# Experts' combining products one pair later, and sums of squares taken by ScalarE, in a two-block network on one core

## The chip, the core and the metric

The kernel is one program on one NeuronCore of a Trainium2 chip. The metric is device time in microseconds (us) of a whole execution; lower is better. TensorE (PE in the profile) does the matrix products, PEld is its weight loading, VectorE is DVE, ScalarE is ACT, GpSimd is POOL, and SyncE (SP) issues most of the transfers between HBM and on-chip memory. TensorE accumulates into eight PSUM banks of 128 partitions by 512 float32.

## The reference

Two blocks on 512 tokens of 1024 numbers. The first block has a hyena mixer and a differential attention mixer; the second has a layer of sparse attentions and a hierarchical mixture of experts, and then a last rmsnorm. The change lies in the mixture of experts and in what surrounds it:

```python
h = rmsnorm_2(x, norm_ffn[l])
x = x + hier_moe(h, ...)            # then rmsnorm_2(x, norm_final)

def hier_moe(h, ...):
    g_logit = tok @ w_group + b_group          # 4 groups
    e_logit = tok @ w_expert + b_expert        # 32 experts, 8 to a group
    # best group, its two best experts, weights from both softmaxes
    ...
    gate, up = jnp.split(xb @ w_gate_up[e], 2, axis=-1)
    return (jax.nn.silu(gate) * up) @ w_down[e]
    # summed per token with the weights
```

All is float32. Each expert has 1024x512 gate-up weights and 256x1024 down weights, so the 32 experts' weights are 96 tiles of 1 MB.

## The kernel before, in words

The program is written as if in one stream; the tile framework gives each operation to its engine, simulates a schedule when the program is built, and from that writes a fixed order of instructions for each engine. Each engine then runs its own order strictly in sequence, and waits by semaphores. `tc.issue_after(ins)` binds what is written inside it to stand behind `ins` in its engine's order. So the orders can move at places that the code's text does not touch.

**Router (lines 1834 to 1946).** Eight steps `m`, one for each block of 128 of the 1024 columns, take the last projection of the attention layer (`pg`, three products of split operands a block) and add the residual into `hn`. The function `after(m)`, called one step late, makes the router's logits (`lg`), transposes `hn` back to rows by token (`tp`), which ScalarE copies into `acc` (the residual stream, 512 tokens in 4 blocks `t` of 128 rows) and VectorE into `xp`, and takes the sums of squares of each token: ScalarE squares `hn` into `sq`, and one-column products with a column of ones (`st`) sum over partitions. Behind the loop, `xd` gets `xp` by four transfers that ScalarE issues (L1871), `rs` is the reciprocal root (VectorE, VectorE, GpSimd, L1876 to 1878), `L` the scaled logits (L1886), and a chain of small VectorE operations picks the group, two experts, ranks `rk` and weights `Wd`. `wr` holds these numbers and `rs` split in a high and a low part (`split`, L328 on ScalarE, L329 on VectorE).

**Experts (lines 1950 to 2060).** 16 pairs of experts (`N_PAIR`), two pairs to a group `g` (`NG` is 8), 64 slots an expert. `prepare(g)` finds which token each slot holds: the one-hot `P`, products `sp` with `wr`, the index `ix`, two gathers `xg` by GpSimd (L1969), and the slot weights `sw`, `sr`. `turn(j)` transposes a pair's rows (`ga`) and scales them into `Xs`. `gate_up(j)` multiplies by the raw weights: the two experts of a pair use the two halves of the array's columns, one 64-wide product each (`gu`, 16 products). `act(j)` transposes the result (`T`) and makes `H`; `down(j)` makes 8 such 64-wide products (`dn`), splits the weighted result into `yh` (ScalarE, L2037) and `yl` (VectorE, L2038), together `Y[j]`, and makes the one-hot `PT[j]` by a product with `sel` (L2041). `combine(g)` brings the outputs of a group's two pairs back to rows by token: 8 blocks of 4 full-width products each (`cb`, L2052), added into `acc` by VectorE (L2055). The `cb` products share two PSUM banks with `sp` and `sel`. The main loop writes, for each pair `j`: `prepare` of the next group (even `j`), `gate_up(j)`, `turn(j+1)`, `down(j-1)`, four blocks of `combine`, `act(j)`; `combine(g-1)` begins in the step that also holds the `down` of its own last pair.

**Weights.** SyncE loads the 96 tiles in order of use (L223, L232); 12 are loaded ahead, and each later one takes a buffer when the products that read it are done.

**Tail.** The last pair's `down`, the last `combine`, then for each block `t` square, power, scale (L2094 to 2097) and the output's transfer. `overflow` (L2106) counts, on VectorE, experts with over 64 tokens, and SyncE reads that count (L2124) for a loop that runs no times with these inputs.

Of the kernel before, what the change touches and what calls it, by code (L numbers as in the profile page):

```python
# [10 lines left out]
FT = mybir.dt.float32  # L11
# [9 lines left out]
D = 1024  # L21
# [1765 lines left out]
def moe(k, A, C, out, ctx, mhp, mh, ml):  # L1787
# [36 lines left out]
    with tc.tile_pool(name="mo1", bufs=2, reuse_waits="tile") as wk, tc.tile_pool(name="mo1x", bufs=1, reuse_waits="tile") as xp, \  # L1824
# [9 lines left out]
        st = pp.tile([128, 4, KD], FT, name="st")  # L1834

        def after(m, hn, hh, hl, sq):
# [12 lines left out]
            xv = xp_[:, :, 512 * h:512 * h + 512].rearrange("p t (a f) -> p t f a", a=4)[:, :, 32 * q:32 * q + 32]  # L1849
            nc.vector.tensor_copy(xv, tp.rearrange("p t (f a) -> p t f a", a=4))  # L1850
        pend = None
        for m in range(KD):
            h2 = wk.tile([128, 512], FT, name="h2", bufs=3)
            nc.scalar.dma_start(h2, k.hdram[:, m, META:])
            if m % 2 == 0:
                wh, wl = k.W.get()
            ps = pp.tile([128, 512], FT, name="pg", bufs=2)
            mm_split(nc, [ps], wh, wl, mh, ml, [slice(0, 512)], KD, slice(128 * (m % 2), 128 * (m % 2) + 128))
            if pend:
                after(*pend)  # L1860
# [7 lines left out]
            pend = (m, hn, hh, hl, sq)  # L1868
# [7 lines left out]
        nc.vector.tensor_reduce(rs, st, AX.X, OP.add)  # L1876
# [50 lines left out]
        nc.vector.tensor_tensor(rk, rk, rp[:, 0:4], OP.add)  # L1927
# [9 lines left out]
        nc.vector.tensor_tensor(Wd, Wd, o2, OP.add)  # L1937
        wp = Wd.rearrange("p t (j e) -> p t j e", e=2)
# [10 lines left out]
    with tc.tile_pool(name="mo2", bufs=2, reuse_waits="tile") as wk, tc.tile_pool(name="mo2y", bufs=1, reuse_waits="tile", side="right") as yp, \  # L1949
# [3 lines left out]
        def prepare(g):  # L1953

            P = wk.tile([128, 4, 4, 64], FR, name="P", bufs=1)
            nc.vector.tensor_tensor(P, rk[:, :, 4 * g:4 * g + 4, None].to_broadcast([128, 4, 4, 64]),
                                    iota[:, None, None, :].to_broadcast([128, 4, 4, 64]), OP.is_equal)
            sp = pp.tile([128, 2, 8], FT, name="cb", bufs=2)
            for j in range(2):
                for t in range(4):  # L1960
                    nc.tensor.matmul(sp[:, j], P[:, t, 2 * j:2 * j + 2].rearrange("p e s -> p (e s)"),
                                     wr[:, t, 2 * g + j], start=(t == 0), stop=(t == 3))
            s8 = wk.tile([128, 2, 8], FT, name="s8")
            nc.vector.tensor_copy(s8, sp)
            ix = wk.tile([128, 2], I32, name="ix")
            nc.vector.tensor_copy(ix, sp[:, :, 6])
            for j in range(2):
                x = XG[2 * g + j] = wk.tile([128, D], FT, name="xg", bufs=3)
                nc.gpsimd.indirect_dma_start(out=x, out_offset=None, in_=xd[:, :],  # L1969
                                             in_offset=bass.IndirectOffsetOnAxis(ap=ix[:, j:j + 1], axis=0))  # L1970
            s3 = wk.tile([128, 2, 3], FT, name="s3")
            nc.gpsimd.tensor_tensor(s3, s8[:, :, 0:6:2], s8[:, :, 1:6:2], OP.add)
            w, r = (wk.tile([128, 2], FT, name=n, bufs=3) for n in ("sw", "sr"))
            for i, a in enumerate((slice(0, 64), slice(64, 128))):
                nc.gpsimd.tensor_copy(w[a], s3[a, :, i])
            nc.gpsimd.tensor_copy(r, s3[:, :, 2])
            SW[g] = (w, r)
# [23 lines left out]
        def gate_up(j):  # L2001
# [4 lines left out]
            for c in range(2):  # L2006
                ws = [k.W.get_raw() for _ in HALF]
                for a in range(4):
                    kk = 4 * c + a
                    for o, w in zip(HALF, ws):  # L2010
                        nc.tensor.matmul(ps[o], xs[:, kk, o], w[:, a], start=(kk == 0), stop=(kk == 7))  # L2011
            G[j] = wk.tile([128, 512], FT, name="G")
            nc.scalar.activation(G[j], ps, AF.Copy, scale=SW[g][1][:, i:i + 1])

        def act(j):
# [9 lines left out]
            nc.vector.scalar_tensor_tensor(H[j], th, 0.5, tp[:, 2:4], op0=OP.mult, op1=OP.mult)  # L2025

        def down(j):
            ps = pp.tile([128, 2, 512], FT, name="dn")
            h = H.pop(j)
            ws = [k.W.get_raw() for _ in HALF]  # L2030
# [4 lines left out]
            w = SW[j // 2][0][:, j % 2:j % 2 + 1]  # L2035
            yh, yl = (yp.tile([128, 2, 512], FR, name=n, bufs=3) for n in ("yh", "yl"))
            nc.scalar.activation(yh, ps, AF.Copy, scale=w)  # L2037
            nc.vector.scalar_tensor_tensor(yl, ps, w, yh.bitcast(FT), op0=OP.mult, op1=OP.subtract)  # L2038
            Y[j] = (yh, yl)
# [3 lines left out]
            nc.vector.tensor_scalar(PT[j], b, col64, None, op0=OP.is_equal)  # L2043

        def combine(g):
            for t in range(4):
                for i in range(2):
                    ps = pp.tile([128, 512], FT, name="cb", bufs=2)
                    n = 0
                    for j in (2 * g, 2 * g + 1):  # L2050
                        for y in Y[j]:
                            nc.tensor.matmul(ps, PT[j][:, t * 128:t * 128 + 128], y[:, i], start=(n == 0), stop=(n == 3))  # L2052
                            n += 1
                    a = acc[:, t, 512 * i:512 * i + 512]
                    nc.vector.tensor_tensor(a, a, ps, OP.add)  # L2055
                    yield

# [7 lines left out]
        for j in range(N_PAIR):  # L2065
# [10 lines left out]
            steps(nxt, 2)  # L2076
            steps(comb, 4)
            act(j)
# [3 lines left out]
        for _ in combine(NG - 1):  # L2082
            pass


    with tc.tile_pool(name="mo3", bufs=2, reuse_waits="tile") as wk:
# [13 lines left out]
        overflow(k, A, rt, cm, rk, Wd, rs, cnt, xd, acc, last_norm)  # L2100


def overflow(k, A, rt, cm, rk, Wd, rs, cnt, xd, acc, last_norm):
# [4 lines left out]
    nc.vector.tensor_scalar(x, cnt, 64.0, None, op0=OP.is_gt)  # L2108
# [128 lines left out]
```

## Time and profile before

| what | value |
| --- | --- |
| time, median of 3 executions | 2403.26 us (2397.03 to 2406.48) |
| profiled execution | 2399.58 us, its span 2397.8 us |
| TensorE busy over the span | 94% |
| VectorE, ScalarE, GpSimd busy | 64%, 45%, 30% |
| granted TensorE clock, mean | 0.965 of full speed |
| HBM traffic over the span | 278.19 MB read, 25.58 MB written |

The profile is one execution recorded in hardware. Times count from the start of its span. A product of two float32 operands stands in it as two records, so `gu` and `dn` groups count two records a product, while `cb` (operands rounded for the fast float32 form) has one; a few records are missing. "A <- B" in the waits means that A waited and B's end released it. The rows that follow further down are from the last 400 us, the only part in which the two kernels differ.

### The profile page before, as it was taken

How to read it: one execution, taken by the hardware profiler on the slowest of the kernel's cores; microseconds unless marked ns; L12 is line 12 of the kernel's file. 1: busy time of each engine (PE TensorE's matmuls, PEld its weight loads, DVE VectorE, ACT ScalarE, POOL GpSimd, SP SyncE). 2: the span in 40 equal slices, each digit the busy share in tenths (PEclk: the TensorE clock that was granted, in tenths of full speed). 3: DMA queues.
4: the chain of work that ended last, by engine and by line, in shares of the span. 5: the costliest groups of instructions: out<-in, count | busy, mean ns of one | idle time of the engine just before them, and what ended most of it. 6: DMA issues, size and time to landing. Idle time of an engine off the chain costs nothing. (4 is left out here: it accounts for less than half of the span.)

```text
span 2397.8 us, 37215 instructions
## 1 busy us (share of the span) xinstructions
PE 2258.6 (94%) x14396; PEld 1844.0 (77%) x14396; DVE 1536.0 (64%) x2845; ACT 1068.5 (45%) x2164; POOL 710.5 (30%) x709
## 2 busy tenths in 40 slices
PE   7999999998999989999999989899999999799997
PEld 6989999997889888888898869887666667344333
DVE  7778764537985587787767744678678554433333
ACT  5666654433344466566656644435444432121111
POOL 3455540115642333333323325432011021101000
PEclk9999999999999899999999989898999999799998
DMA  6333322223127422111111225532121336699871
GB/s 225 125 108 111 113 93 89 88 71 105 56 85 217 142 62 71 53 54 53 58 49 54 71 89 173 179 82 64 62 75 53 115 103 236 254 423 372 330 299 45
DMA packets 242061, 306.19 MB, mean 128 GB/s; under 512 B 20648, under 2 KB 208436, under 8 KB 233306
## 3 DMA queue, kind: packets, MB, share of 16 engines
q1 hardware_dynamic: 203328, 245.90, 30.6%
q10 hardware_dynamic: 33002, 32.64, 4.5%
q0 software_dynamic: 5552, 25.25, 2.9%
q8 instruction: 114, 1.87, 0.3%
q14 instruction: 65, 0.53, 0.1%
HBM read 278.19 MB, written 25.58 MB: 127 GB/s over the span
## 5 line engine op out<-in xcount | busy, mean ns | idle before, releaser
L263 POOL TENSOR_TENSOR wlo<-wraw,whi 128x1024 fp32r<-128x1024 f32 (+1 forms) x91 | 181.0, 1997 | 479.2 <-ACT whi L282 346.7
L263 DVE TENSOR_TENSOR wlo<-wraw,whi 128x1024 fp32r<-128x1024 f32 (+2 forms) x201 | 225.5, 1135 | 148.7 <-ACT whi L282 141.1
L282 ACT CAST whi<-wraw 128x1024 fp32r<-128x1024 f32 x198 | 206.0, 1047 | 169.9 <-PE ps L813 50.2
L811 PE MATMUL ps<-xh,whi 128*128 128x264 f32 x1024 | 214.0, 286 | 3.4 <-ACT hTd L584 3.0
L813 PE MATMUL ps<-xl,whi 128*128 128x264 f32 x1024 | 213.9, 286 | 0.0
L815 PE MATMUL ps<-xh,wlo 128*128 128x264 f32 x1024 | 211.8, 285 | 0.0
L811 PE MATMUL pj<-xh,whi 128*128 128x512 f32 (+2 forms) x544 | 193.9, 359 | 5.0 <-DVE rr L1193 4.6
L815 PE MATMUL pj<-xh,wlo 128*128 128x512 f32 (+2 forms) x544 | 191.2, 354 | 0.5 <-DVE wlo L263 0.5
L813 PE MATMUL pj<-xl,whi 128*128 128x512 f32 (+2 forms) x544 | 191.4, 354 | 0.0
L811 PEld LDWEIGHTS ps<-xh,whi 128*128 128x128 f32 x1024 | 160.5, 189 | 5.8 <-ACT hTd L584 4.0
L813 PEld LDWEIGHTS ps<-xl,whi 128*128 128x128 f32 x1024 | 161.2, 189 | 1.6 <-issue 1.3
L815 PEld LDWEIGHTS ps<-xh,wlo 128*128 128x128 f32 x1024 | 160.8, 189 | 1.2 <-issue 0.8
L813 PE MATMUL pj<-vx,whi 128*128 128x256 f32 (+1 forms) x480 | 136.6, 286 | 0.0
L1302 ACT ACTIVATE p<-S,mx 128x528 f32<-128x528 f32 x128 | 89.6, 702 | 77.5 <-DVE mx L1300 42.6
L811 PEld LDWEIGHTS pj<-xh,whi 128*128 128x128 f32 x544 | 104.8, 193 | 19.9 <-DVE rr L1193 6.0
L815 PEld LDWEIGHTS pj<-xh,wlo 128*128 128x128 f32 x544 | 104.0, 192 | 13.7 <-DVE wlo L263 0.7
L813 PEld LDWEIGHTS pj<-xl,whi 128*128 128x128 f32 x544 | 104.4, 193 | 12.6
L2011 PE MATMUL gu<-wraw,Xs 128*64 128x512 f32 x400 | 112.1, 626 | 0.0
L1300 DVE TENSOR_REDUCE mx<-S 128x1 f32<-128x528 f32 x128 | 88.9, 700 | 13.6 <-PE S L1299 12.2
L2055 DVE TENSOR_TENSOR acc<-acc,cb 128x512 f32<-128x512 f32 x64 | 43.1, 684 | 79.6 <-PE cb L2052 79.4
L813 PEld LDWEIGHTS pj<-vx,whi 128*128 128x128 f32 x480 | 91.6, 191 | 0.0
L1298 PE MATMUL S<-ks,qh 128*128 128x264 f32 x256 | 71.9, 301 | 11.9 <-ACT p L1302 11.7
(662 smaller groups left out, 6482.7 us busy)
## 6 DMA issues: line engine op xcount, KB each, us to landing
wraw<-in_w_gate_up_dram SPq DMA_DIRECT2D x50, 1024.0 KB
wraw<-in_hy_w_in_dram SPq DMA_DIRECT2D x32, 1024.0 KB
wraw<-in_da_w_in_dram SPq DMA_DIRECT2D x32, 1024.0 KB
wraw<-in_hy_w_out_dram SPq DMA_DIRECT2D x16, 1024.0 KB
wraw<-in_da_w_out_dram SPq DMA_DIRECT2D x16, 1024.0 KB
wraw<-in_w_down_dram SPq DMA_DIRECT2D x14, 1024.0 KB
wraw<-in_w_in_dram SPq DMA_DIRECT2D x20, 512.0 KB
whi<-in_w_down_dram SPq DMA_DIRECT2D x18, 512.0 KB
```

Of the source, the lines that this page charges most:

```text
L263: eng.tensor_tensor(l, r, h.bitcast(FT), OP.subtract)
L282: nc.scalar.copy(hf, vf)
L811: nc.tensor.matmul(ps[i], wh[:, kk, fsl], xh[:, kk, c], start=f, stop=False)
L813: nc.tensor.matmul(ps[i], wh[:, kk, fsl], xl[:, kk, c], start=False, stop=False)
L815: nc.tensor.matmul(ps[i], wl[:, kk, fsl], xh[:, kk, c], start=False, stop=l)
L1298: nc.tensor.matmul(S[:, i, 0:TH], qh[:, qs], ks[:, c], start=True, stop=False)
L1300: nc.vector.tensor_reduce(mx[:, m:m + 1], S[:, :, 0:TH], AX.XY, OP.max, negate=True)
L1302: nc.scalar.activation(p.rearrange("p (a b) -> p a b", a=2), S[:, :, 0:TH], AF.Exp, bias=mx[:, m:m + 1], accum_out=sm[:, m:m + 1])
L2011: nc.tensor.matmul(ps[o], xs[:, kk, o], w[:, a], start=(kk == 0), stop=(kk == 7))
L2055: nc.vector.tensor_tensor(a, a, ps, OP.add)
```

## The change

Six edits, all in the mixture of experts and its edges:

1. The `st` products and the eight squarings of `hn` go. ScalarE squares `acc` by token instead, with a running sum: four blocks of 896 columns ahead of the last `after`, four of 128 behind it; one addition replaces the reduction.
2. VectorE's part of the split of `rs` stands behind the ranks.
3. `prepare(0)` works by pair: half of `P`, its products, its index, its gather, then the other half. Its small sums go to VectorE.
4. In the main loop the four blocks of `combine` are bound behind the last product of `gate_up(j)` and written ahead of `down(j-1)`, so `combine(g-1)` begins one pair later. In `down` the `sel` product comes first and the loop's order is by output half; the last pair's `yh` and `yl` are made in halves.
5. `last_combine` takes eight PSUM banks: pair 14's products of the eight blocks ahead of pair 15's.
6. The overflow count's VectorE operations are bound behind `H[4]`.

```diff
-        st = pp.tile([128, 4, KD], FT, name="st")
+        st = xp.tile([128, 2, 4], FT, name="st")
+        def squares(i, c):
+            for t in range(4):
+                sq = wk.tile([128, D], FT, name="sq")
+                nc.scalar.activation(sq[:, 0:c.stop - c.start], acc[:, t, c], AF.Square, accum_out=st[:, i, t:t + 1])
...
-                nc.tensor.matmul(st[:, i, m:m + 1], sq[:, c], k.ones, start=True, stop=True)
...
-            sq = wk.tile([128, 512], FT, name="sq")
-            nc.scalar.activation(sq, hn, AF.Square)
...
+        squares(0, slice(0, D - 128))
         after(*pend)
+        squares(1, slice(D - 128, D))
...
-        nc.vector.tensor_reduce(rs, st, AX.X, OP.add)
+        nc.vector.tensor_tensor(rs, st[:, 0], st[:, 1], OP.add)
...
-        rsb = rs[:, :, None].to_broadcast([128, 4, N_PAIR])
-        split(k, rsb, wr[:, :, :, 4], wr[:, :, :, 5])
+        with tc.issue_after(last_rank.ins):
+            split(k, rsb, wr[:, :, :, 4], wr[:, :, :, 5])
...
+            for js in ((0,), (1,)) if g == 0 else ((0, 1),):
...
+            eng = nc.gpsimd if g else nc.vector
+            eng.tensor_tensor(s3, s8[:, :, 0:6:2], s8[:, :, 1:6:2], OP.add)
...
-            for a in range(2):
-                for i in range(2):
-                    for o, w in zip(HALF, ws):
-                        nc.tensor.matmul(ps[o, i], h[:, a, o], w[:, a, 512 * i:512 * i + 512], start=(a == 0), stop=(a == 1))
+            for i in range(2):
+                for a in range(2):
+                    for o, wt in zip(HALF, ws):
+                        nc.tensor.matmul(ps[o, i], h[:, a, o], wt[:, a, 512 * i:512 * i + 512], start=(a == 0), stop=(a == 1))
+                if last or i:
+                    c = slice(i, i + 1) if last else slice(0, 2)
+                    nc.scalar.activation(yh[:, c], ps[:, c], AF.Copy, scale=w)
...
+        def last_combine():
+            banks = []
+            for n, b in (("gu", 2), ("gu", 2), ("ga", 1), ("T", 1), ("cb", 2), ("cb", 2)):
+                ps = pp.tile([128, 512], FT, name=n, bufs=b)
+                t, i = divmod(len(banks), 2)
+                add(ps, t, i, N_PAIR - 2, True, False)
+                banks.append(ps)
...
-            gate_up(j)
+            done = gate_up(j)
             nxt = turn(j + 1) if j + 1 < N_PAIR else iter(())
-            steps(nxt, 1)
+            with tc.issue_after(done):
+                steps(comb, 4)
             if j:
                 down(j - 1)
             if i == 0 and g:
                 comb = combine(g - 1)
-            steps(nxt, 2)
-            steps(comb, 4)
-            act(j)
+            steps(nxt, 3)
+            hidden = act(j)
+            if j == 4:
+                late = hidden
...
-        for _ in combine(NG - 1):
-            pass
+        last_combine()
...
+    with tc.issue_after(late):
+        nc.vector.tensor_scalar(x, cnt, 64.0, None, op0=OP.is_gt)
```

Two places show how the engines' orders move. The first is TensorE's order late in the expert stage of before, from the transposes of one pair's hidden values (`T`) over the last seven down products of the pair before it to the first combining products that read those down products (`cb<-yh`, `cb<-yl`):

```order
L1994 MATMUL ga<-ident,xg 128x128 x4
L2034 MATMUL dn<-wraw,H 64x512
L2020 MATMUL T<-ident,G 128x128 x4
L2034 MATMUL dn<-wraw,H 64x512 x7
L2011 MATMUL gu<-wraw,Xs 64x512
L2052 MATMUL cb<-yh,PT 128x512 x2
L2052 MATMUL cb<-yl,PT 128x512 x2
L2011 MATMUL gu<-wraw,Xs 64x512 x7
L2052 MATMUL cb<-yh,PT 128x512
L2052 MATMUL cb<-yl,PT 128x512
```

The same stretch in the changed kernel, from the seven down products of the same kind to the first combining products that read them:

```order
L2053 MATMUL dn<-wraw,H 64x512 x7
L2041 LDWEIGHTS sel
L2041 MATMUL cb<-rkT,sel 128x512
L2022 MATMUL gu<-wraw,Xs 64x512 x8
L2053 MATMUL dn<-whi,H 64x512 x2
L2053 MATMUL dn<-wlo,H 64x512 x2
L2053 MATMUL dn<-whi,H 64x512 x2
L2053 MATMUL dn<-wlo,H 64x512 x2
L2022 MATMUL gu<-wraw,Xs 64x512 x8
L2062 MATMUL cb<-yh,PT 128x512
L2062 MATMUL cb<-yl,PT 128x512
```

Before, one gate-up product stood between the two; now sixteen gate-up and eight down products do, in runs of eight rather than of one and seven.

The second place is ScalarE's order at the end of the router loop, before:

```order
L328 CAST hh<-hn 128x512
L1867 ACTIVATE sq<-hn 128x512
L1847 COPY acc<-tp 128x4x128 x2
L1880 COPY lgs<-lg 36x512
L1871 DMA xd<-xp 128x1024 x4
L328 CAST wr<-rs 128x64
```

and in the changed kernel:

```order
L328 CAST hh<-hn 128x512
L1852 COPY acc<-tp 128x4x128 x2
L1840 ACTIVATE sq,st<-acc 128x896 x2
L1885 COPY lgs<-lg 36x512
L1840 ACTIVATE sq,st<-acc 128x896
L1876 DMA xd<-xp 128x1024 x2
L1840 ACTIVATE sq,st<-acc 128x896
L1876 DMA xd<-xp 128x1024 x2
L1840 ACTIVATE sq,st<-acc 128x128 x4
L328 CAST wr<-rs 128x64
```

Eight squarings and the four transfers' issues now stand between the last copy into `acc` and `rs`.

## Rows read from the trace of the kernel before

**Rows 1.** The page: the span and its instructions.

```profile
span 2397.8 us, 37215 instructions
```

**Rows 2.** Busy time by stage: busy us (instructions) of each engine, PEclk, DMA share, GB/s.

```profile
2000.00:2039.10 39.10, 39.10 (x209) 31.60 (x208) 13.38 (x16) 10.41 (x17) 2.40 (x1) 1.00 0.58 211
...
2068.30:2210.40 142.10, 142.10 (x629) 59.70 (x628) 50.18 (x97) 27.70 (x56) 14.97 (x28) 0.99 0.96 386
2210.40:2367.00 156.60, 147.88 (x580) 58.41 (x579) 51.92 (x93) 26.09 (x49) 6.31 (x12) 0.98 0.69 260
```

**Rows 3.** The chain that ended last, 2300 to 2324 us: start, us, what.

```profile
2300.35 1.12 ACT yh L2037
...
2301.50 1.29 DVE yl L2038
...
2303.57 5.27 PE gu L2011 x14
2308.84 1.13 PE cb L2052 x4
2309.97 1.00 PE dn L2034 x2
...
2312.11 1.87 PE dn L2034 x8
...
2316.16 2.04 PE cb L2052 x8
...
2320.33 3.58 PE gu L2011 x14
```

**Rows 4.** Waits, 2068 to 2370 us: us in total, times, longest.

```profile
PE cb L2052 <- ACT yh L2037: 4.8, 4, 1.2
...
PEld cb L2052 <- DVE acc L2055: 4.1, 5, 0.8
...
PEld gu L2011 <- DMA wraw<-in_w_down_dram: 0.4, 1, 0.4
```

**Rows 5.** Timeline of the router's end: start, us, engine; in brackets the idle time before.

```profile
2040.43 0.63 ACT L1867 ACTIVATE sq<-hn 128x512 f32<-128x512 f32 x1
...
2040.96 1.07 ACT L1847 COPY acc<-tp 128x512 f32<-128x512 f32 x2
...
2041.42 0.95 PE L1844 MATMUL st<-ones,sq 128*128 128x1 f32 x8
...
2043.36 0.15 DVE L1876 TENSOR_REDUCE rs<-st 128x4 f32<-128x32 f32 x1
...
2043.54 2.77 ACTq L1871 DMA_DIRECT2D xd<-xp  x4
...
2046.69 0.28 DVE L329 TENSOR_TENSOR wr<-rs,wr 128x64 fp32r<-128x64 f32 x1 [0.88 <-ACT wr L328]
```

**Rows 6.** Timeline from the first gather to the first gate-up product.

```profile
2057.48 1.18 POOL L1972 TENSOR_TENSOR s<-s 128x6 f32<-128x6 f32 x1 [12.64 <-DVE ix L1966]
...
2065.84 0.19 POOL L1972 TENSOR_TENSOR s<-s 128x6 f32<-128x6 f32 x1
...
2068.27 1.12 PE L2011 MATMUL gu<-wraw,Xs 128*64 128x512 f32 x2
```

**Rows 7.** Timeline of the tail.

```profile
2366.97 0.75 PE L2020 MATMUL T<-ident,G 128*128 128x128 f32 x4
...
2377.47 1.06 ACT L2094 ACTIVATE s<-acc 128x1024 f32<-128x1024 f32 x1 [3.52 <-DVE acc L2055]
...
2378.44 0.19 ACT L2094 ACTIVATION_READ_ACCUMULATOR s<-acc 128x1 f32 x1
...
2388.51 1.28 DVE L2097 SCALAR_TENSOR_TENSOR s<-acc,rf,gf 128x1024 f32<-128x1024 f32 x1 [0.66 <-POOL rf L2096]
```

**Rows 8.** Transfers of SyncE's queue after the first buffer came free.

```profile
2073.57 1.05 SPq L232 DMA_DIRECT2D wraw<-in_w_gate_up_dram  x2
```

**Rows 9.** Busy time and transfer rate within the expert stage, columns as in group 2.

```profile
2080.00:2200.00 120.00, 120.00 (x538) 52.49 (x534) 45.70 (x85) 23.98 (x47) 9.06 (x14) 1.00 1.01 414
```

More of the change, by code (lines that the diff above doesn't have):

```diff
@@ L1963, in prepare @@
             s8 = wk.tile([128, 2, 8], FT, name="s8")
-            nc.vector.tensor_copy(s8, sp)
[L1965 to L1970, printed above, removed]
+            ix = wk.tile([128, 2], I32, name="ix")
@@ new lines, in prepare @@
+            for js in ((0,), (1,)) if g == 0 else ((0, 1),):
+                c = slice(2 * js[0], 2 * js[-1] + 2)
+                n = c.stop - c.start
+                nc.vector.tensor_tensor(P[:, :, c], rk[:, :, 4 * g + c.start:4 * g + c.stop, None].to_broadcast([128, 4, n, 64]),
+                                        iota[:, None, None, :].to_broadcast([128, 4, n, 64]), OP.is_equal)
+                for j in js:
+                    for t in range(4):
+                        nc.tensor.matmul(sp[:, j], P[:, t, 2 * j:2 * j + 2].rearrange("p e s -> p (e s)"),
+                                         wr[:, t, 2 * g + j], start=(t == 0), stop=(t == 3))
+                c = slice(js[0], js[-1] + 1)
+                nc.vector.tensor_copy(ix[:, c], sp[:, c, 6])
+                for j in js:
+                    x = XG[2 * g + j] = wk.tile([128, D], FT, name="xg", bufs=3)
+                    nc.gpsimd.indirect_dma_start(out=x, out_offset=None, in_=xd[:, :],
+                                                 in_offset=bass.IndirectOffsetOnAxis(ap=ix[:, j:j + 1], axis=0))
@@ L1976, in prepare @@
-            nc.gpsimd.tensor_copy(r, s3[:, :, 2])
+                eng.tensor_copy(w[a], s3[a, :, i])
+            eng.tensor_copy(r, s3[:, :, 2])
             SW[g] = (w, r)
@@ L2043, in down, with add @@
             nc.vector.tensor_scalar(PT[j], b, col64, None, op0=OP.is_equal)
+            ps = pp.tile([128, 2, 512], FT, name="dn")
+            h = H.pop(j)
+            ws = [k.W.get_raw() for _ in HALF]
+            w = SW[j // 2][0][:, j % 2:j % 2 + 1]
+            yh, yl = (yp.tile([128, 2, 512], FR, name=n, bufs=3) for n in ("yh", "yl"))
+            last = j == N_PAIR - 1
+            for i in range(2):
[5 more added lines that the diff above has]
+                    nc.scalar.activation(yh[:, c], ps[:, c], AF.Copy, scale=w)
+                    nc.vector.scalar_tensor_tensor(yl[:, c], ps[:, c], w, yh[:, c].bitcast(FT), op0=OP.mult, op1=OP.subtract)
+            Y[j] = (yh, yl)
+        def add(ps, t, i, j, start, stop):
+            for n, y in enumerate(Y[j]):
+                nc.tensor.matmul(ps, PT[j][:, t * 128:t * 128 + 128], y[:, i], start=(start and n == 0), stop=(stop and n == 1))
         def combine(g):
@@ L2048, in combine @@
                     ps = pp.tile([128, 512], FT, name="cb", bufs=2)
-                    n = 0
                     for j in (2 * g, 2 * g + 1):
-                        for y in Y[j]:
-                            nc.tensor.matmul(ps, PT[j][:, t * 128:t * 128 + 128], y[:, i], start=(n == 0), stop=(n == 3))
-                            n += 1
+                        add(ps, t, i, j, j % 2 == 0, j % 2 == 1)
                     a = acc[:, t, 512 * i:512 * i + 512]
@@ L2056, in combine @@
                     yield
+        def last_combine():
[5 more added lines that the diff above has]
+                banks.append(ps)
+            ps = None
+            for t in range(4):
+                if t == 3:
+                    ps = pp.tile([128, 2, 512], FT, name="dn")
+                    banks += [ps[:, i] for i in range(2)]
+                    for i in range(2):
+                        add(banks[6 + i], t, i, N_PAIR - 2, True, False)
+                for i in range(2):
+                    add(banks[2 * t + i], t, i, N_PAIR - 1, False, True)
+                    a = acc[:, t, 512 * i:512 * i + 512]
+                    nc.vector.tensor_tensor(a, a, banks[2 * t + i], OP.add)
         def steps(g, n):
@@ L2099, in moe, with overflow @@
         last_norm()
-        overflow(k, A, rt, cm, rk, Wd, rs, cnt, xd, acc, last_norm)
-def overflow(k, A, rt, cm, rk, Wd, rs, cnt, xd, acc, last_norm):
+        overflow(k, A, rt, cm, rk, Wd, rs, cnt, xd, acc, last_norm, late)
+def overflow(k, A, rt, cm, rk, Wd, rs, cnt, xd, acc, last_norm, late):
     nc, tc = k.nc, k.tc
```

29 lines of the change are left out of this document (7 added, 22 removed).

## The prediction

> **What bounds the kernel now.** The table of busy times by stage comes first, since the two kernels differ only in the last 400 us of the span [rows 1]. In the router stage TensorE is busy in all 39.10 us. In the first half of the expert stage it is busy in all 142.10 us at a granted clock of 0.99, with the transfers' share at 0.96; in the second half in 147.88 of 156.60 us [rows 2]. So TensorE's own order is the bound, weights in HBM stand close behind, and 8.7 us of idle time lie in the second half. The waits say what for: combining products wait for `yh` (4 times, 1.2 us each), and only 0.4 us in all is put down to weights [rows 4].
>
> The chain that ended last gives TensorE's prices [rows 3]. A run of 8 records of down products takes 1.87 us, one of 14 gate-up records 3.58 (16 with the two that the trace lacks). The difference, 1.71 for 8 records, makes 0.854 for 4 records, that is for one product in each column half; the two halves run side by side. 1.87 less two such pairs leaves 0.17: the change from full-width products to column-half ones. The combining products show the same: 8 in 2.04, 4 in 1.13, so 0.23 each and about 0.2 for the change ahead of them. The row to learn from is the down run of 2 records, 1.00 us: one product alone in its half costs the 0.17 and then a whole 0.854, because nobody runs in the other half. Cutting a run of 8 products in 1 and 7 therefore costs one change and one half-empty pair more, 1.00 us in all; I put an odd piece at 0.427 and a change at 0.17.
>
> **Check of these prices.** I walked through TensorE's order of before from the first gate-up product with 0.427 a column-half product, 0.233 a `cb`, 0.107 a transpose, 0.21 a `sel`, 0.1 an `sp` product, and the two charges. From 2068.27 [rows 6] to the ninth pair's transposes the sum is 140.3; the trace has 142.1, the end of the first window [rows 2]. 1.5 of the difference stands in the first gate-up run at a lower clock. To the last pair's transposes at 2366.97 [rows 7] the sum is 282.9, the trace 298.7. So 14.0 us are lost after the ninth pair to something that is no work of TensorE: the 8.7 idle, some 3 in two gate-up runs behind such gaps that were granted less clock (one takes 5.27 instead of 3.58 [rows 3]), the rest in gaps too short for the table.
>
> **The expert stage, work.** The same products counted in both orders, from the first gate-up product to the last combining one: 168 changes of width before, 106 after; 38 odd pieces in 77 runs before, 18 in 47 after. The binding of four combining blocks behind `gate_up` gathers what was strewn: 62 × 0.17 = 10.5, 20 × 0.427 = 8.5, so −19.1 us (row sums 294.5 and 275.5). At the last pair's transposes the sums are 282.9 and 256.9, −26.0; 7 of it comes back behind them, since 20 more combining products (4.7 us) and some changes then stand in the tail.
>
> **The expert stage, waits.** Before, `yh` of the down just finished takes 1.12, then `yl` 1.29 [rows 3], and only one gate-up product stands between that down and the first product that reads them. After, 16 gate-up and 8 down products stand there, some 10.6 us by the prices above, against a chain of 2.4. So these waits go, and nothing takes their place in the order: what is late next is an accumulation bank, for the `acc` addition (0.8 us at the longest, 4.1 in all now [rows 4]). Between the first block of a bound group and the third, which needs its bank, lie another block and transposes or a down product, 1.6 to 3 us, more than an addition behind one other VectorE operation takes. I walked both orders with all engines' rows: it stalls in before at the places where the trace does, and in after twice, 0.4 each. That takes the 14.0 to 0.8 (bounds: 0.8, and 3.9 if the two low-clock runs stay). At the last transposes −26.0 − 13.2 = −39.2, or −36.1.
>
> **The tail.** Before, 2366.97 to 2389.79, the end of the last scaling [rows 7], is 22.8. After it carries the 4.7 and two changes more, and its products in eight banks cover the wait for the last `yh` and `yl`. My walk gives 28.0, so +5.2 (bounds +2 and +6). What follows the last scaling is the same in both. Sum for experts and tail: −34.0, or −30.9.
>
> **The router.** Before, 8 one-column records a block; in the one run that stands alone 8 take 0.95 [rows 5]. Six of eight blocks stand ahead of the last projection product, where TensorE never rests [rows 2]: 6 × 0.95 = −5.7 at the most, half of it if they hide under the transposes between them; I take −4. The squares of 512 columns (0.63 each) leave ScalarE, off its path. Against that, ScalarE's queue behind the last copy into `acc`. That copy ends at 2042.03 and `rs` starts at 2043.36, 1.33 later [rows 5]. After, four squares of 896 stand there, each 1.16 × 7/8 ≈ 1.04 from the row of 1024 with its read of the sum [rows 7], the copy of the logits (512 columns, at 0.6 as the square of 512), four issues of `xd` (2.77 together [rows 5]) and four squares of 128 at about 0.35 to 0.4: 4.2 + 0.6 + 2.8 + 1.5 = 9.1, less 1.33: +7.7. All of the routing and so the first gather queue behind `rs`; TensorE has nothing else to do there. That this undoes the gain of the first edit is the part of the change I am surest of. Two edits give some back: VectorE no longer waits 0.88 + 0.28 for ScalarE's half of the split of `rs` [rows 5], −1.1; and the first gather no longer stands behind GpSimd's sum of 1.18 (the same operation takes 0.19 where VectorE does not build `P` beside it [rows 6]), half of the position products, 0.9, and the count's operations, −2.3. Router: −4 + 7.7 − 1.1 − 2.3 = +0.3; bounds −4 and +5.
>
> The count moved behind `H[4]` costs VectorE some 3 us where it is busy a third of the time; SyncE's reading of it stands behind a load that waits for a later down product, so I cost it at nothing. If SyncE did stop there, later loads would start by as much later.
>
> **Sum.** −34.0 or −30.9, +0.3: −32 to −34, I take −33. Span 2397.8 − 33 = 2364.8, execution 2399.6 − 33 = 2366.6. The profiled execution lies 3.7 below the median, so against that: 2403.3 − 33 = 2370.
>
> **Rivals.** *Weights become the bound.* 12 of 96 tiles are in before 2073.57, when the first freed buffer is loaded [rows 8]; 84 tiles of 1.0486 MB and 14 gathers of 0.524 remain, 95.4 MB. At 414 GB/s, which stood from 2080 to 2200 [rows 9], they take 230 us and end at 2304; at the 386 of the whole first half [rows 2], 247 us and 2321. The last transposes come at about 2328 and the last down needs its tile at 2330. So the margin is 9 to 26 us. Each per cent under that 386 is 2.5 us more; at a tenth under it the end is 2348, 18 late: gain 15, time 2388. For it: loads now wait for TensorE, and a faster TensorE takes that slack. Against it: 0.4 us of waiting for weights so far. The Trainium skill, page "DMA: Bandwidth & Descriptors", section "Specifications", puts HBM to one core at about 358 GB/s; by it the last tile would land at 2340 and the time would be about 2380. This trace's 414 over 120 us stands against that limit.
>
> *The bound groups wait (slower side).* In before a combining block could stand anywhere; in after four are bound together over two banks, with two joins a pair, 28 in all. If VectorE, behind `yl` (1.29) or scalings, adds late at each join, TensorE waits there. From 33/28 = 1.2 us a join there is no gain; at 2 us it is +23 and 2426. For it, those 4.1 us in five waits; against it, VectorE is busy 50 of 142 us [rows 2].
>
> *The clock and the router.* The gaps go but low-clock runs remain or come elsewhere, and the router costs its full +5: gain 20 to 26, time about 2380.
>
> *The waits only move.* Row sums fall by 19 but stalls of some 14 arise behind `Xs` or `G` in the denser order: gain 19, time 2384.
>
> **Chances.** The forecast (2360 to 2378) 0.64; weights 0.10; clock or router 0.10; moved waits 0.06; bound groups that cost over half of the gain 0.07, more than half of them not faster at all; better than 2358 0.03. The range 2356 to 2388 leaves out little beyond the bound groups and the tail of the weights. A measurement of this kernel tells about 0.5%, 12 us, from no change: faster 0.90, same 0.06, slower 0.04.
>
> **What would show it.** Right: no wait of `cb` for `yh` or `yl` over 0.5 us; `dn` x2 pieces of 1.00 gone from most of the chain; the last pair's transposes about 260 us behind the first gate-up product (298.7 before); `rs` some 9 us behind the last `acc` copy and the first gate-up product within 4 us of 2068. Wrong: gate-up or down waiting for transfers by several us at a time, or `cb` waiting for `acc` additions at most joins.

## The result, and the profile after

The changed kernel takes 2363.97 us in the median (2362.28 to 2370.13, 4 runs) against 2401.17 for the kernel before (2397.03 to 2406.48, 4 runs): a ratio of 0.9849, 95% interval 0.9821 to 0.9876. That is 37 us less, inside the forecast range; the forecast was 2370, 33 less. A later measurement of the same two kernels (`changed_again` below) gave 2368.19 against 2400.30, 32 us less, so the size of the gain is known to some 5 us.

The page of the changed kernel begins so:

```profile
span 2360.5 us, 37091 instructions
```

Both spans can be cut at the same places of the program. Each length is the difference of two starts (or ends) of rows in the timelines: the first and the eighth `hn` of the router, the scaling of `rs`, the first gather, the first gate-up product, the last pair's transposes `T`, the end of the last output scaling, the end of the span.

| stretch | before | after | difference |
| --- | --- | --- | --- |
| start to first `hn` (same code) | 1991.7 | 1991.9 | +0.2 |
| first to eighth `hn` | 47.4 | 42.9 | -4.5 |
| eighth `hn`'s end to scaling of `rs` | 3.75 | 7.64 | +3.9 |
| `rs` to first gather | 15.3 | 12.6 | -2.7 |
| first gather to first gate-up | 9.4 | 10.6 | +1.2 |
| first gate-up to last `T` | 298.7 | 259.4 | -39.3 |
| last `T` to last scaling's end | 22.8 | 26.4 | +3.6 |
| rest | 8.0 | 8.4 | +0.4 |

The busy times by stage of the changed kernel, cut at the first gate-up product, at the ninth pair's region and at the last transposes; these answer to [rows 2]:

```profile
2000.00:2034.70 34.70, 34.70 (x161) 26.88 (x160) 12.88 (x16) 7.73 (x12) 2.40 (x1) 1.00 0.67 247
2066.25:2208.00 141.75, 141.44 (x655) 61.82 (x656) 55.29 (x119) 30.16 (x59) 14.11 (x25) 0.99 0.98 403
2208.00:2325.60 117.60, 117.57 (x528) 52.93 (x525) 44.72 (x82) 24.10 (x45) 6.12 (x12) 1.00 0.81 323
2325.60:2352.10 26.50, 18.77 (x79) 11.64 (x77) 18.33 (x29) 6.14 (x11) 2.17 (x4) 0.94 0.18 66
```

In the second half TensorE now works 117.57 of 117.60 us, at full granted clock. The 8.7 us of idle time are gone, and with them the low clock (0.98 in the second half before, 1.00 now). In the list of waits from 2066 to 2326 us no wait of a combining product (L2062) for `yh`, `yl` or `acc` is left. What is left are short waits of weight loads (PEld), of which only the three in the first line below are for a transfer, and one wait of a product itself, 0.3 us for `G`:

```profile
PEld dn L2053 <- DMA wraw<-in_w_gate_up_dram: 0.9, 3, 0.4
...
PE T L2032 <- ACT G L2024: 0.3, 1, 0.3
```

The chain that ended last, of the changed kernel, in the same phase as [rows 3]:

```profile
2210.11 3.43 PE dn L2053 x16
2213.55 3.43 PE gu L2022 x16
2216.98 2.07 PE cb L2062 x8
2219.05 0.47 PE T L2032 x4
2219.51 1.85 PE cb L2062 x8
...
2233.45 1.00 PE dn L2053 x2
...
2236.06 3.58 PE dn L2053 x14
```

Here a down run of 16 records follows a gate-up run and takes 3.43, with no change of width ahead of it, and the combining products stand in eights. Pieces of 1.00 are left, but few. No ScalarE or VectorE row stands in this part of the chain.

At the router's end ScalarE does what was foreseen, in its timeline (answering to [rows 5]), but faster:

```profile
2036.07 1.07 ACT L1852 COPY acc<-tp 128x512 f32<-128x512 f32 x2
2037.02 0.96 ACT L1840 ACTIVATE sq<-acc 128x896 f32<-128x896 f32 x1
...
2038.78 0.33 ACTq L1876 DMA_DIRECT2D xd<-xp  x1
...
2039.37 0.95 ACT L1840 ACTIVATE sq<-acc 128x896 f32<-128x896 f32 x1
...
2040.39 1.15 ACTq L1876 DMA_DIRECT2D xd<-xp  x1
2041.15 0.20 ACT L1840 ACTIVATION_READ_ACCUMULATOR sq<-acc 128x1 f32 x1
2041.59 0.31 ACT L1840 ACTIVATE sq<-acc 128x128 f32<-128x128 f32 x1 [0.25 <-ACT sq L1840]
```

The issues of `xd` lie beside the squares. The last of them runs from 2040.39 over 1.15 us, and the engine is idle 0.25 us in all of that time.

### The profile page after: what moved, and what is told of

Read it like the earlier page. It is cut to its first block, busy times and chain, and to the rows that moved or that the text cites. A ratio compares the mean times of both kernels' runs of the same rounds, so it can differ in the third digit from the quotient of the medians.

```text
span 2360.5 us, 37091 instructions
## 1 busy us (share of the span) xinstructions
PE 2219.6 (94%) x14332; PEld 1832.0 (78%) x14332; DVE 1537.9 (65%) x2852; ACT 1070.5 (45%) x2173; POOL 706.2 (30%) x705
## 3 DMA queue, kind: packets, MB, share of 16 engines
q8 instruction: 113, 1.85, 0.3%
## 5 line engine op out<-in xcount | busy, mean ns | idle before, releaser
L2022 PE MATMUL gu<-wraw,Xs 128*64 128x512 f32 x400 | 97.3, 604 | 0.0
L1298 PE MATMUL S<-ks,qh 128*128 128x264 f32 x256 | 72.0, 302 | 11.9 <-ACT p L1302 11.7
L1656 ACT ACTIVATE P<-S,mx 128x128 f32<-128x128 f32 (+3 forms) x96 | 50.3, 530 | 70.1 <-PE pt L1673 55.3
```

The source lines that it names most:

```text
L1298: nc.tensor.matmul(S[:, i, 0:TH], qh[:, qs], ks[:, c], start=True, stop=False)
L1656: nc.scalar.activation(p[:, m, 0:n], S[:, m, 0:n], AF.Exp, bias=mx[:, m:m + 1], accum_out=sm[:, m:m + 1])
L2022: mm = nc.tensor.matmul(ps[o], xs[:, kk, o], w[:, a], start=(kk == 0), stop=(kk == 7))
```

## The experiments

Times are medians; the kernel before ran beside each group: 2401.25 for the first four, 2402.77 for the next four, 2400.56 and 2400.30 for the last two groups. "Lengths" are those of the table above, from one profile each. In all kernels the start up to the first `hn` is the same code, yet it took 1989.3 to 2000.8 us from profile to profile. That spread is larger than many effects here, so effects under 5 us are read from lengths. A second profile of the changed kernel (`changed_again`) shows how well these repeat: 7.66, 12.57, 10.65, 260.25, 26.45 and 8.40 for the third to the last stretch, so 0.1 in most and 0.9 in the expert stage. That 0.9 is the granted clock in the first 10 us of the gate-up products: 0.86 in the first profile and 0.77 in the second, with TensorE busy throughout.

**Which edit carries the gain: `loop_only`**

```diff
 (kernel before)
...
-            gate_up(j)
+            done = gate_up(j)
...
-            steps(nxt, 1)
+            with tc.issue_after(done):
+                steps(comb, 4)
...
-            steps(nxt, 2)
-            steps(comb, 4)
+            steps(nxt, 3)
```

> The kernel before with the main loop's edit alone (combining blocks bound behind gate_up and begun one pair later); router, start, down and tail as before. Theory: nearly the whole gain is this edit. Its TensorE order has a row sum of 275.1 us from the first gate-up product (before 294.5, changed kernel 275.5) and 256.9 at the last pair's transposes, so these should stand 258 to 261 us behind the first gate-up product, against 298.7 and 259.4, and the time at 2366 to 2369. Rival: router, start or tail carry a good part of the 37 us; then 2375 or more.

Measured 2371.34 (ratio 0.9883, 0.9847 to 0.9919); its profiled execution 2363.43, its lengths 259.83 from the first gate-up product to the last `T` and a tail of 25.6. As the theory had it by lengths: this edit alone is -38.9 and +2.8, so 36.1 of the 37.3 us. By medians it is 30 us; the median lies 2 us above the expected 2369, which is less than the spread of the start, and the interval alone (2364 to 2382) would not rule out the rival's 2375. The lengths do.

**What in that edit: `unbound` and `bound_early`**

```diff
 (changed kernel: unbound)
-            with tc.issue_after(done):
-                steps(comb, 4)
+            steps(comb, 4)
```

> The changed kernel with the four combining blocks written at the same place but not bound behind gate_up's last product. Its order strews them as before: 165 changes of width, 42 odd pieces, row sum 295.7 (changed kernel 106, 18, 275.5), and the first combining products stand right behind the down that they read. Theory (cuts and waits, both of the order): the last transposes at 295 to 299 us behind the first gate-up product, time 2395 to 2398. Rival A (that the code begins the combine one pair later does it): 2364 to 2370. Rival B (cuts alone, no waits): 2384.

Measured 2400.07 (0.9992, 0.9971 to 1.0013): as slow as before. First gate-up to last `T` 301.4, some 2 us over what was expected. Writing the combine ahead of the down gains nothing by itself; only with the binding does it. Its chain that ended last is that of the kernel before again:

```profile
2212.14 3.15 PE dn L2053 x13
2215.29 0.01 PE gu L2022
2215.29 0.44 PE dn L2053
2215.73 0.02 issue
2215.75 1.12 ACT yh L2056
2216.88 0.02 issue
2216.90 1.29 DVE yl L2057
```

```diff
 (changed kernel: bound_early)
-            with tc.issue_after(done):
-                steps(comb, 4)
             if j:
                 down(j - 1)
             if i == 0 and g:
                 comb = combine(g - 1)
+            with tc.issue_after(done):
+                steps(comb, 4)
```

> The changed kernel with the blocks bound behind gate_up, but written behind down as before, so that a combine reads the output of the down just made. Row sum 282.3 (126 changes, 26 odd pieces), 6.8 above the changed kernel, and six waits for yh and yl of about 2 us. Theory (waits and cuts both count): 17 us slower than the changed kernel, 20 if gate-up runs behind the waits get less clock: 2381 to 2384. Rival A (cuts alone): 2371. Rival B (waits alone): 2374 to 2377.

Measured 2386.76 (0.994, 0.9918 to 0.9963), 23 above the changed kernel's median; by lengths 284.2, 24.8 more, with a tail 3.4 shorter: 21 us. Its waits from 2066 to 2340 us:

```profile
PE cb L2062 <- ACT yh L2056: 4.2, 4, 1.2
PE cb L2062 <- DVE yl L2057: 2.9, 5, 0.6
```

The row sum to the last `T` (268.8 against 256.9) gives 11.9 of the 24.8. Of the other 12.9, 7.0 are idle time of TensorE (7.3 us in the stretch against 0.3 in the changed kernel); the rest, part of it lower clock (0.98 against 0.99 over the stretch), was not taken apart. Cuts alone and waits alone are both too small; the theory was some 3 us low.

**Waits alone, the cuts left: `no_wait`**

```diff
 (kernel before)
-                        for y in Y[j]:
+                        for y in Y[2 * g]:
```

> The kernel before, but both halves of a combine read the first pair's yh and yl, so nothing waits for the down just made (this leaves the second pair's outputs out of the sum). Its order has as many cuts as before: 157 changes, 42 odd pieces, row sum 294.4 against 294.5. Theory: only waits go, so 8 to 11 us off the kernel before, 2390 to 2393. Rival A (cuts alone make the difference between the two kernels): 2401, as before. Rival B (the waits are worth all 37): 2364 to 2370.

Measured 2391.18 (0.9967, 0.995 to 0.9984), 10 less than before, with as many cuts. Of the waits of TensorE for `yh` and `yl` this is left:

```profile
PE cb L2052 <- ACT yh L2037: 1.2, 2, 0.6
```

In the stretch from the first gate-up product to the last `T` TensorE is idle 2.8 us instead of 8.7. The busy times of that stretch, of the kernel before and then of `no_wait`:

```profile
2068.27:2366.97 298.70, 289.98 (x1208) 118.11 (x1207) 102.11 (x190) 53.79 (x105) 21.31 (x40) 0.98 0.82 320
```

```profile
2068.95:2362.11 293.16, 290.37 (x1228) 124.64 (x1228) 106.39 (x195) 53.44 (x105) 21.34 (x40) 1.00 0.83 326
```

The stretch is only 5.5 shorter, and the tail 4.6 (18.2 against 22.8). But the order moved too, since the last group's combining products no longer need the last pair's outputs: 12 of them stand behind the last `T` instead of 32, so 20 more, 4.7 us at 0.233, are done ahead of it. With these the waits are worth some 10 us in the stage. Both rivals fall: the waits are worth 10 of 37.

**The price of a cut: `halves_apart`**

```diff
 (changed kernel)
-                for a in range(2):
-                    for o, wt in zip(HALF, ws):
+                for o, wt in zip(HALF, ws):
+                    for a in range(2):
```

> The changed kernel with the products of each down in the order half A, half A, half B, half B for each output half instead of A, B, A, B. The work is the same. Theory (a product runs beside its neighbour in the order only if that is in the other half, each takes 0.854): a run of 8 takes 4.27 us instead of 3.41, 13.7 us over 16 downs, less 1.4 for a slightly better order: 2376. Rival A (halves run side by side only where they alternate strictly): about 2405 to 2417. Rival B (the hardware takes products of the free half out of order): 2363.

Measured 2373.55 (2 runs); by lengths first gate-up to last `T` is 266.66, 7.3 more than in the changed kernel, though the row sum without the effect is 1.3 lower: 8.6 over 15 downs, 0.57 each, between the expected 0.85 and nothing. The chain shows why:

```profile
2205.48 1.86 PE dn L2053 x4
...
2208.95 3.58 PE dn L2053 x12
...
2218.56 0.42 PE gu L2022
2218.98 3.00 PE dn L2053 x14
...
2221.99 0.42 PE dn L2053
2222.41 3.43 PE gu L2022 x15
```

A down alone between full-width work takes 1.86 + 3.58 = 5.44, against 1.00 + 3.58 in the same place of the changed kernel: 0.86 more, one product, as priced. A down between two gate-up runs pays about half of it: in this chain the gate-up run of 14 records, the down of 16 and the gate-up run of 16 take 10.45 us (2215.40 to 2225.85), and by the prices 9.99 without the effect. At both ends of that down the rows of 0.42 alternate between down and gate-up, so its first and last product run beside a gate-up product. Both rivals fall; "an odd piece costs 0.427" holds where full-width work stands on both sides.

**The weights: `no_low`**

```diff
 (changed kernel)
-            for n, y in enumerate(Y[j]):
-                nc.tensor.matmul(ps, PT[j][...], y[:, i], start=(start and n == 0), stop=(stop and n == 1))
+            nc.tensor.matmul(ps, PT[j][...], Y[j][0][:, i], start=start, stop=stop)
```

> The changed kernel without the combining products of yl (leaves out the low part of the split). TensorE's row sum falls from 275.5 to 251.2, the last transposes from 256.9 to 239.2. Theory: weights still come in time (in the changed kernel the last load is issued at 2298 and at 420 GB/s all loads could end sooner), so about 24 us faster, 2338 to 2343. Rival: transfers become the bound; TensorE waits several us for weights and the time is 2346 to 2356.

Measured 2352.34 (2 runs), the rival's time, but not by its mechanism. By lengths: 246.1 and a tail of 23.4, so 13.3 + 3.0 = 16.3 gained of 24.3 us of work. Waits for weights stay small in the whole stage, though the transfers run at their highest rate for 190 us:

```profile
PEld dn L2053 <- DMA wraw<-in_w_gate_up_dram: 1.5, 5, 0.4
...
PEld gu L2022 <- DMA whi<-in_w_gate_up_dram: 0.5, 2, 0.2
```

Its busy times in two windows, with clock, transfers' share and GB/s at the end:

```profile
2110.00:2210.00 100.00, 98.54 (x444) 40.22 (x444) 46.74 (x102) 22.45 (x44) 10.40 (x18) 1.00 1.02 423
2210.00:2300.00 90.00, 89.11 (x395) 35.66 (x391) 37.05 (x70) 20.07 (x39) 6.13 (x12) 1.00 1.02 423
```

3.6 of the missing 8 us are in the tail, where VectorE's additions and the norm set the end; 4.4 are in the expert stage. There TensorE is idle 2.7 us instead of 0.3, most of it in short waits on VectorE and ScalarE, and the first 10 us were granted 0.74 of the clock instead of 0.86, which is 1.2 us; about 1 us is left unexplained.

**The four smaller edits: `old_squares`, `old_start`, `old_tail`, `squares_early`**

```diff
 (changed kernel: old_squares)
+                nc.tensor.matmul(st[:, i, m:m + 1], sq[:, c], k.ones, start=True, stop=True)
...
+            nc.scalar.activation(sq, hn, AF.Square)
...
-        squares(0, slice(0, D - 128))
...
-        squares(1, slice(D - 128, D))
...
 (changed kernel: old_start)
-        with tc.issue_after(last_rank.ins):
-            split(k, rsb, wr[:, :, :, 4], wr[:, :, :, 5])
...
+        split(k, rsb, wr[:, :, :, 4], wr[:, :, :, 5])
...
-            for js in ((0,), (1,)) if g == 0 else ((0, 1),):
+            for js in ((0, 1),):
...
-            eng = nc.gpsimd if g else nc.vector
+            eng = nc.gpsimd
 (changed kernel: old_tail)
-            last = j == N_PAIR - 1
+            last = False
...
-        last_combine()
+        for _ in combine(NG - 1):
+            pass
 (changed kernel: squares_early)
...
-        squares(0, slice(0, D - 128))
+            if m == 5:
+                squares(0, slice(0, 512))
+            if m == 7:
+                squares(1, slice(512, D - 256))
         after(*pend)
-        squares(1, slice(D - 128, D))
+        squares(2, slice(D - 256, D))
...
```

> The changed kernel with the sums of squares by one-column products again. The two traces put these products at 5.2 us of TensorE up to the last hn, and the squares on ScalarE at 3.9 us more between that hn and rs. Theory: 1.3 us slower than the changed kernel, 2365. Rival (the forecast's price of the queue on ScalarE, 7.7 us): 2 to 3 us faster, 2361.

> The changed kernel with the first prepare in one piece, its small sums on GpSimd, and the split of rs at its old place. The two traces show 2.7 us less from rs to the first gather, of which 1.2 is lost again before the first gate-up product; the order's row sum rises by 2.2. Theory: 2 to 4 us slower, 2366 to 2368. Rival: nothing, as another engine ends last there: 2364.

> The changed kernel with the last group's combine in two banks and the last yh and yl whole. The tail's TensorE work is the same; walking the order gives 1 us less than with eight banks, not counting that the clock fell in the tail of before. Theory: within 2 us of the changed kernel, 2363 to 2366. Rival (eight banks are worth the wait for the last yl and the low clock behind it): 4 to 6 us slower, 2368 to 2370.

> The changed kernel with ScalarE's squares in three parts: 512 columns inside the step of block 5, 256 in that of block 7, only the last 256 behind the last copy. ScalarE is idle in three quarters of the router stage. Theory: rs comes about 3 us sooner behind the last hn, less 1 us for a slightly worse order of the expert stage: 2361 to 2362. Rival (the logits' copy and the issues of xd set the end there): no change, 2364.

Medians 2366.91, 2367.76, 2363.86 and 2359.09, ratios 0.9847, 0.9864, 0.9854 and 0.9831, each interval within 0.0022 of its ratio: none is clear of the changed kernel. The lengths follow (`first to eighth hn` is compared between profiles of equal clock there, see the last section; other columns as in the table above). The last column is the granted clock in the first 10 us from the first gate-up product on; TensorE is busy in all of that time, so 0.1 of the clock there is 1 us of the column "to last `T`".

| kernel | `hn` to `hn` | to `rs` | to gather | to gate-up | to last `T` | tail | clock |
| --- | --- | --- | --- | --- | --- | --- | --- |
| changed, 2 profiles | 42.9, 41.3 | 7.6, 7.7 | 12.6 | 10.6 | 259.4, 260.3 | 26.4 | 0.86, 0.77 |
| old_squares | 45.9 | 3.8 | 12.6 | 8.8 | 258.7 | 26.5 | 1.00 |
| old_start | 42.9 | 7.6 | 13.3 | 9.6 | 262.1 | 26.5 | 0.85 |
| old_tail | 41.3 | 7.6 | 12.6 | 10.1 | 260.4 | 25.6 | 0.75 |
| squares_early | 41.3 | 4.1 | 12.6 | 10.4 | 261.6 | 26.5 | 0.75 |

Two of the windows behind the last column, of the changed kernel and then of `old_squares`:

```profile
2066.30:2076.30 10.00, 10.00 (x43) 3.35 (x44) 2.16 (x4) 1.03 (x3) 2.40 (x6) 0.86 0.56 193
```

```profile
2071.60:2081.60 10.00, 10.00 (x49) 3.55 (x50) 2.93 (x6) 1.43 (x4) 3.93 (x8) 1.00 0.62 212
```

The squares by product cost 4.5 up to the last `hn` (45.9 against 41.3) and give 3.9 back at `rs`; that nearly evens out. Behind it `old_squares` is ahead by 1.8 before the first gate-up product and by 0.7 to 1.6 in the expert stage, so that its length in all is 2 to 3 us less than that of the changed kernel. The 0.7 to 1.6 are less than the clock alone gives (1.4 and 2.3 us by the last column), and some 0.6 of the 1.8 is probably the clock's too: the eight position products ahead of the gate-up run (`cb`, L1967 there and L1972 in the changed kernel) take 1.22 us instead of 1.85. Whether the edit or chance gave that profile the better clock, one profile does not tell. So neither the theory's 1.3 us slower nor the rival's 2 to 3 us faster is shown; the queue on ScalarE costs 3.9, as the traces had said. In `old_start` the gather comes 0.7 later and the gate-up products follow 1.0 sooner, so the edits to the start bring nothing there; what they bring, some 2.6 us at equal clock, comes out of a different order of the expert stage (2.2 by the row sum). The eight banks of the tail cost 0.8. `squares_early` takes 3.6 off the way to `rs` and loses 2.2 in the expert stage against the first profile, 1.1 of it by the clock and 1.1 by the order, as its row sum has it; it comes out 1.5 to 2.5 ahead.

**Eight blocks instead of four: `eight_bound`**

```diff
 (squares_early)
-                steps(comb, 4)
+                steps(comb, 8 if i else 0)
```

> The kernel of squares_early with all eight combining blocks of a group bound behind one gate_up instead of four behind each of two. The cuts fall: row sum 273.4 against 276.5, 12 odd pieces against 20, and 255.2 against 258.0 at the last transposes. But eight blocks over two banks in one go, and what else stands there, queue VectorE: the walk over all engines' rows gives some 8 us of waits for additions and for Xs, which squares_early does not have. Theory (fewer cuts are lost again to waits): 2 to 5 us slower than squares_early, last transposes 264 to 267 us behind the first gate-up product (261.6). Rival (cuts alone): 3 us faster, 258.5.

> The changed kernel once more, beside eight_bound on one chip, for the spread of its stages from one profile to the next. Theory: 2364, the last transposes 259 to 260.5 us behind the first gate-up product, the tail 26.4, rs 7.4 behind the last hn.

Measured 2370.45 and 2368.19 (0.9871 and 0.9861). The last `T` of `eight_bound` stands 269.9 behind the first gate-up product, 8.3 more than in `squares_early` with 2.8 us less work by the row sum. Its waits, from 2066 to 2330 us:

```profile
PE gu L2026 <- ACT Xs L1998: 2.7, 3, 0.9
PE T L2036 <- ACT G L2028: 1.2, 4, 0.3
PE cb L1976 <- DVE acc L2075: 0.9, 2, 0.5
```

TensorE is idle 6.0 us in the stretch, against 0.5 in `squares_early`:

```profile
2063.32:2333.23 269.91, 263.87 (x1182) 113.83 (x1182) 100.41 (x200) 52.89 (x104) 20.22 (x37) 0.98 0.88 352
```

So 5.5 of the 11 us lost (8.3 and the 2.8) are idle time; the rest was not taken apart. In its outcome this is the forecast's slower rival, met at eight blocks: a larger bound group holds up what stands behind it. Its mechanism, late additions, shows only in part: products wait 0.9 us for `acc`, and most of their waits are for `Xs` and `G`. That the additions in VectorE's queue delay `Xs` was argued from the order, not shown. At four blocks only 0.3 us of such waits appears, for `G`. The theory had the sign; its size was 3 to 6 us low.

## Why the prediction was right, step by step

**Work of TensorE.** It rests on a price for each product, change of width and odd piece, and on counts from the two orders. The last `T` was to stand 39.2 us earlier behind the first gate-up product (36.1 with low-clock runs left); it stands 39.3 earlier, and no low-clock run is left behind the ninth pair. That the two agree to 0.1 us is luck: the second profile of the changed kernel has 38.5, by the clock of its first 10 us. The row sum runs 1.3 us short at the first `T` and 2.5 at the last, so the same prices hold through the whole stage. In the kernel before the shortfall rises from 1.8 at the ninth pair to 15.8 at the last [rows 7]. `no_wait` puts 10 us on waits with the cuts kept, `bound_early` splits its 24.8 about in halves, and `unbound` has both back. These three show that cuts and waits each count; the sum of 26 and 13 was not taken apart further than that. The lower end of the prediction's sum, -30.9 and +0.3, is -30.6 and not -32; nothing hangs on it.

**Waits.** That `yh` and `yl` no longer end any wait was right, and that no other wait takes their place also. Where waits come back is shown by `bound_early` (for `yh` and `yl`) and by `eight_bound` (for `Xs` and `G`).

**The router was mis-sized: +0.3 forecast, -2.2 measured.** The term "+7.7" for ScalarE's queue failed. The way from the last copy into `acc` to `rs` was to take 9.1 us instead of 1.33 and takes 5.8 (2037.14 to 2042.90), so +4.4; with the 0.5 that the copy itself comes sooner, since no squaring of `hn` stands ahead of it, +3.9. The term charged ScalarE with 2.77 us for the four issues of `xd`; the changed kernel's rows show them beside the squares, with 0.25 us of idle engine. The -4 for the one-column products measured -4.5. So the statement that the queue undoes the gain of the first edit holds only nearly: 0.6 us of the gain is left instead of a loss of 3.7.

The "-1.1 and -2.3" for the start measured -2.7 to the first gather, and 1.2 of it is lost again before the first gate-up product, for which the prediction had no term; why, stays open. The rows tell where the 2.7 come from. 0.9 lies ahead of the first `P`: before, ScalarE's half of the split of `rs` starts at 2046.35, when the issues of `xd` end, though `rs` is there at 2044.83; in the changed kernel the issues stand ahead of `rs`, and it starts at once. The two rows, before and after:

```profile
2046.35 0.30 ACT L328 CAST wr<-rs 128x64 fp32r<-128x64 f32 x1 [2.88 <-DMA xd<-xp]
```

```profile
2044.40 0.30 ACT L328 CAST wr<-rs 128x64 fp32r<-128x64 f32 x1 [1.53 <-POOL rs L1883]
```

`old_start`, which has the split at its old place, keeps this 0.9, so it comes from the new place of the issues and not from the second edit. 1.3 lie between `P` and the index `ix`: `old_start` keeps 0.5, the time by which `ix` came behind its products (2056.84 to 2057.31) while VectorE worked on the overflow count, and lacks 0.8, which is what working by halves gives. The last 0.5 lie between `ix` and the gather, where GpSimd's sum stood [rows 6].

**The tail: +5.2 forecast, +3.6 measured.** Of combining products 56 stand behind the last `T` in the changed kernel's trace and 32 in that of before: 24 more, 5.6 us at 0.233, where the prediction counted 20 and 4.7. The time from the last `T` to the end of the last combining product grows by only 1.9 us, since before TensorE was idle 2.4 us of it and was granted 0.81 of the clock, and now 1.5 us and full clock. The two windows, before and after:

```profile
2366.97:2385.25 18.28, 15.88 (x53) 9.24 (x52) 9.87 (x16) 4.95 (x8) 1.14 (x2) 0.81 0.16 57
```

```profile
2325.63:2345.83 20.20, 18.74 (x79) 11.64 (x77) 12.63 (x23) 4.31 (x8) 0.65 (x2) 1.00 0.08 27
```

From there to the end of the last scaling it takes 6.2 us instead of 4.5. `loop_only` and `old_tail`, without the eight banks, have 21.2 and 4.4 there: the banks end the last product 1.0 sooner, but VectorE then makes seven additions one behind the other (2340.78 to 2345.04) ahead of the norm's first small operation. So they cost 0.8 and did not earn their place.

**Rivals.** Weights did not become the bound: 0.9 us of waiting. Transfers ran at 423 GB/s, above the 414 of [rows 9], as the busy times of the changed kernel from 2110 to 2230 us show:

```profile
2110.00:2230.00 120.00, 119.97 (x563) 56.37 (x561) 54.05 (x115) 24.46 (x48) 12.58 (x21) 1.00 1.02 423
```

The Trainium skill gives a limit of 358 GB/s to a core ("DMA: Bandwidth & Descriptors", Specifications). The 423 GB/s over 120 us stand above it, so it did not bind here. The last load was issued at 2298.39 in the changed kernel's timeline, 27 us ahead of the last `T`:

```profile
2298.39 0.80 SPq L223 DMA_DIRECT2D wlo<-in_w_down_dram  x2
```

**The signs named ahead.** No wait of `cb` for `yh` or `yl`, few pieces of 1.00, the last `T` 259.4 us behind the first gate-up product and that product at 2066.25 came as said. One sign did not: `rs` stands 5.8 us behind the last `acc` copy and not some 9.

## What to carry to other kernels

Price an engine's order, not only its work: count how often products of another shape cut a run, and how often a run with two halves is cut at an odd place; here 62 changes and 20 odd pieces were worth about 19 us with the same products. Look for a product that stands right behind the chain that makes its operand, and move it one unit of work later by binding it in the order; writing it later in the code was not enough. The size of a bound group is to be tried: with four blocks over two banks no product waited for a bank, with eight TensorE was idle 5.5 us more. And before a difference of 1 or 2 us between two profiles is put down to an edit, compare the granted clock of the same stretch in both.

## What the runs showed that was not expected

The router's first two blocks have two lengths. TensorE waits there 2.0 us for the first `hn` in both profiles of the changed kernel (2.03 and 2.01 ahead of the first `tp`). Behind that wait one was granted 0.83 of the clock over the next 10 us, with 0.51, about the lower of its two levels (1.2 and 2.4 GHz), from 1994.0 to 1997.4; the other, of the same code, was granted full clock. The length to the eighth `hn` is 42.9 and 41.3. The first window is of the first profile, the second of `changed_again`:

```profile
1991.90:2002.00 10.10, 9.38 (x38) 7.40 (x39) 4.82 (x6) 2.24 (x4) 2.00 (x1) 0.83 1.03 414
```

```profile
2000.80:2011.00 10.20, 9.47 (x45) 7.38 (x46) 6.29 (x8) 2.93 (x5) 2.02 (x1) 1.00 1.03 415
```

So of two equal stretches one can differ by 1.5 us through the clock alone, which is about as much as a small edit is worth here. And a transfer's issue by ScalarE can lie beside its own arithmetic: in the changed kernel the four issues leave the engine idle 0.25 us. Before, where no arithmetic was under way, the same four held ScalarE's next operation up by 1.5 us (2044.83 to 2046.35).
